# Hybrid decoder block: a new written order for all engines up to the first attention step, with one pair's weight sums on VectorE

## Chip, cores, metric

One core of one Trainium2 chip. The metric is the device time of one execution in microseconds (us). The engines are named as in the profile: PE (TensorE), DVE (VectorE), ACT (ScalarE), POOL (GpSimd), SP (SyncE, which issues the DMAs).

## The reference

One decoder layer on a 1024 x 1024 float32 input, one batch:

```python
h = rmsnorm(x, mix_norm_g[l])
proj = h @ w_in[l]
qa, ka, va, q_lat, kv_lat, k_r, g_a, g_b = jnp.split(proj, IN_OFFSETS, axis=-1)
qa = apply_rope(qa.reshape(B, S, SWA_HEADS, HEAD_DIM), cos_a, sin_a)
ka = apply_rope(ka.reshape(B, S, SWA_KV_HEADS, HEAD_DIM), cos_a, sin_a)
o_a = swa_sink_attention(qa, ka, va, swa_sinks[l])        # 8 heads of 64, window 128
cq = rmsnorm(q_lat, q_norm_g[l])                          # 384 wide
ckv = rmsnorm(kv_lat, kv_norm_g[l])                       # 256 wide
...
y = jax.nn.sigmoid(g_a) * (o_a @ w_o_swa[l]) + jax.nn.sigmoid(g_b) * (o_b @ w_o_mla[l])
x = x + y @ w_out[l]
h = rmsnorm(x, ffn_norm_g[l])
x = x + (jax.nn.silu(h @ w_gate[l]) * (h @ w_up[l])) @ w_down[l]
return rmsnorm(x, final_norm_g)
```

`o_b` is latent attention over `cq` and `ckv` with a separate rotary key.

## The kernel before

**Arithmetic.** Every float32 factor is split into a high part and a low part. ScalarE writes the high part (a copy or cast), VectorE the low part (the value minus the high part). `mm3` (L164 to L170) then runs three matmuls for each block of 128 rows: high by high (L168), high by low (L169 or L170, by operand) and low by high. In the large products, a 2 x 2 arrangement of half matrices is computed with seven products instead of eight, in the order 1, 6, 2, 7, 5, 4, 3. That needs sums and differences of weight tiles (`lat_mix`, `lat_mix2`, and in class `Seven` `mix` and a part of `prep`), which GpSimd makes, and of activation tiles ("sets": `set_sub` on VectorE, `set_four` on GpSimd). A product is 12 matmuls of 512 columns.

**Stages.** First comes the projection to the local attention's queries, keys and values (`nat`, L505 to L516: 8 row blocks, two column groups, two parts of 12 matmuls of 336 columns each). For each block, `square` takes the sum of squares on ScalarE and a 128 x 128 diagonal `dg` of the norm factors on GpSimd (L438), `spread` multiplies it with ones on TensorE (`rb`, L442), and `normalize` multiplies the transposed block on VectorE (L445). Behind the projection `row_act` and `row_dve` (L472, L479) apply the rotation; the five VectorE instructions of the latter are the lines L489 to L498 and two of L173 and L176. Then come the latent projections: three pairs j = 0, 1, 2 of seven products each (tiles `fa`, `fb`, weights `wr`, sums `sm`, split weights `wl`; casts at L871, low parts at L873). Then the gates (class `Seven`, object `gates`) are woven into 16 steps of local attention (`for it in range(N_SW)`): query transposes `qT`, scores `sc`, softmax, transposes of the probabilities `pT`, values. Behind these lie latent attention, the output product and the feed-forward part.

**What sets the order.** The string `ROWS` is an order written out by hand for all five engines. It is executed while the kernel is built, one step after the other, and each engine runs its instructions in just this order. A step is two letters and indices; `STEPS` (L1031) maps the letters to functions: `nt` nat, `xs`/`xt` loads, `sq` square, `sp` spread, `nm` normalize, `qh`/`ql` high and low part of a normalized block, `ho` its store, `ra`/`rd` rotation on ScalarE and VectorE, `qo` store of the queries, `sl` load of a set, `ss` its three subtractions, `sf` set_four, `sh`/`so` high and low part of a set's tile, `la`/`sc` load and scale of latent weights, `mx`/`my` the two parts of their sums, `lh`/`ll` high and low part of latent weights, `mm` a latent product, `ev` its copy out of the accumulator, `es` its square sum, `rh`/`rl`/`ro` split and store of a result, `kr` the rotary key, `kl` load of the keys, `gl`/`gs`/`gm`/`gp` load, scale, sums and preparation of the gates' weights, `wq`/`wt`/`ws` load, transposes and scores of an attention step. An engine that reaches an instruction whose operand is late waits there, and all that stands behind it on that engine waits too. Behind `ROWS` the attention loop and what follows run in the order of the code; `lat_tail` puts the latent results' norms between the loop's steps by their number, the first of it, `lat_stats`, with 32 matmuls of one column (`st`, L1053).

Of the kernel before, what the change touches and what calls it, by code (L numbers as in the profile page):

```python
# [8 lines left out]
F32 = mybir.dt.float32  # L9
# [8 lines left out]
P = 128  # L18
# [69 lines left out]
def hybrid_block_kernel(  # L88
# [475 lines left out]
    def set_four(c):  # L564
        if c // 2 not in t4_raw:
            t4_raw[c // 2] = U("h4", F32, (P, 2, 4, P))
        r, t = h_set[c]
        for k in range(0, 4, 2):
            k = slice(k, k + 2)
            sub(t4_raw[c // 2][:, c % 2, k], r[:, 1, k], t[:, 1, k], nc.gpsimd)  # L570
# [6 lines left out]
        sq0 qh2 xs2 sq1 ql2 nt110 xt7 ra0 xs4 qh3 sp0 rd0 nt111 xt4 sp1 ra1 ql3 xt5 nt200 sq2 qo0 nm0 nt201 xs3 rd1  # L577
        qh0 xs6 nt210 sq4 xs7 ql0 sp2 nt211 xt6 nm2 xs5 nm1 sp4 ra2 nt300 ho2 sq3 nm4 nt301 sq6 qo1 rd2 ho4 qh4 nt310
        ho0 qh2 ql4 la10 qh1 sp6 nt311 ql2 sq5 qo2 ho1 ql1 nt400 ra3 sq7 rd3 sp5 nt401 nm5 qo3 sp7 nt410 tb nm7 qh5
        ho5 sc10 nt411 nm6 ho7 ql5 qh6 ho6 sp3 nm3 qh7 nt500 la01 ra4 ql7 qh3 ho3 nt501 lh11 ql6 sl1 nt510 ll11 rd4  # L580
        sl2 nt511 ql3 nt600 ra5 sc01 qo4 rd5 la00 nt601 sl0 ns ss1 nt610 la11 nt611 sh12 sf1 ss2 qo5 sl3 nt700 ra6
        so12 sh22 sf2 sc00 rd6 nt701 mx0 nt710 ss0 qo6 sc11 nt711 so22 sh02 so02 ra7 lh01 rd7 sf0 ll01 mx1 ph qo7 sh23
        ss3 sh14 mm01 sh13 sh03 sh21 so23 sh31 sh32 so13 mm11 kt1 ev01 so03 lh06 so32 sh33 sf3 ll06 sh01 sh04 so31
        mm06 lh02 so01 lh07 ll02 ev11 so04 sh34 my0 sh11 so34 mm02 lh05 ev06 sh24 ll07 so33 so11 la20 mm07 ev02 so21
        es02 ll05 lh16 so14 ll16 la21 mm05 lh03 ev07 ll03 so24 kt0 mm16 lh04 ev05 ll04 kr05 sc20 mm03 lh12 ev16 rh05
        sc21 ll12 mm04 rl05 my1 ev03 ro05 lh21 es03 ll21 mx2 mm12 lh17 ev04 ll17 kr04 gl00 mm21 lh22 ll22 rh04 ev12
        rl04 es12 my2 mm17 ev21 ro04 lh26 rh12 ll26 rl12 mm22 lh15 ev17 ro12 gs00 ll15 wq0 kl gp1 mm26 ev22 lh27 es22
        ll27 rh22 rl22 mm15 lh13 ev26 ll13 gl01 mm27 lh25 ev15 ro22 ll25 es15 rh15 mm13 wq1 ev27 rl15 lh14 ro15 ll14
        wt0 lh23 ev13 gl10 mm25 ll23 rh13 es13 rl13 gs01 mm14 ev25 ro13 lh24 gm0 es25 ll24 mm23 ev14 es14 rh14 rl14
        ws0 ev23 ro14 es23 mm24 gp2 gp3 rh23 rr rl23 ev24 ro23 es24  # L590
    """

    class Seven:


        def __init__(self, pairs, ms, load, done, ahead, load_at, mix_at, head=(), at=None, scale=None, scale_at=(), piece=4, vec=()):


            self.pairs, self.ms, self.load, self.done = pairs, ms, load, done
            self.n_ahead = ahead  # L600
            j0 = 1 + max((j for j, _ in head), default=-1)
            order = list(head) + [(j, q) for j in range(j0, pairs) for q in ORDER]
# [9 lines left out]
            self.scaled = set()  # L612
            self.scale = scale
# [32 lines left out]

        def prep(self, j, q, m):
# [5 lines left out]
            if q == 7:  # L653
                a12, s1 = self.part(j, m, 1, 0), self.sums[(j, m)][:, 1]
                for k in range(0, 4, self.piece):
                    k = slice(k, k + self.piece)
                    sub(a12[:, k], a12[:, k], s1[:, k], nc.gpsimd)
# [14 lines left out]
        def run(self):  # L672
            j, q, m = self.seq[self.n_run]
# [8 lines left out]
            if q == 6:  # L682
# [4 lines left out]
                go_on=q in (2, 7, 4, 3))  # L687
            if q == 1:
                self.tmp[(j, m)] = U("pu", F32, (P, 2, 512))
# [12 lines left out]
            return j, q, m  # L702
# [41 lines left out]
    def sw_qT(it):  # L744
# [5 lines left out]
        ptq = ptq.bitcast(F32)  # L750
        qs = U("qs", F32R, (P, 2, 2, P))
        e, o = qs[:, :, 0], qs[:, :, 1]
        nc.scalar.copy(e[0:64], ptq[0:64])
        nc.scalar.copy(o[64:128], ptq[64:128])
        nc.vector.tensor_tensor(e[64:128], ptq[0:64], e[0:64].bitcast(F32), op=ALU.subtract)
        nc.vector.tensor_tensor(o[0:64], ptq[64:128], o[64:128].bitcast(F32), op=ALU.subtract)
        d["qs"] = qs

    def sw_scores(it):
        g, b = divmod(it, NB)  # L760
        d = sw[it]
        qs = d.pop("qs")
        c0 = P if b == 0 else 0
        kc = slice((b - 1) * P + c0, (b + 1) * P)
        mx = tiny("mx", 4)
        scs = []
        for hp in range(2):
            sc = PX("sc", (P, 2, 2 * P))
            scs.append(sc)
            for j in range(2):  # L770
                nc.tensor.matmul(sc[:, j, c0:], qs[:, hp, j], khd[g][0][:, kc], start=True, stop=False)
                nc.tensor.matmul(sc[:, j, c0:], qs[:, hp, j], khd[g][1][:, kc], start=False, stop=True)
            for j in range(2):
                h = 2 * hp + j
                nc.vector.tensor_tensor_reduce(sc[:, j, c0:], sc[:, j, c0:], band[:, c0:], 1.0, NEG, op0=ALU.add,
                                               op1=ALU.max, accum_out=mx[:, h:h + 1])
# [4 lines left out]
        nc.vector.tensor_tensor(es, nm, ns, op=ALU.subtract)  # L781
        den = tiny("den", 4)
# [16 lines left out]
        d["kbs"] = [1] if b == 0 else [0, 1]  # L799

# [47 lines left out]
    def lat_mix(j):  # L848
        a11, a21, a22 = lraw[(j, 0)][:, :, 0], lraw[(j, 0)][:, :, 1], lraw[(j, 1)][:, :, 1]
        t = lsum[j] = U("sm", F32, (P, 2, 4, P))  # L850
        for k in range(0, 4, 2):
            k = slice(k, k + 2)
            add(t[:, 0, k], a21[:, k], a22[:, k], nc.gpsimd)
            sub(t[:, 1, k], t[:, 0, k], a11[:, k], nc.gpsimd)
            sub(a21[:, k], a11[:, k], a21[:, k], nc.gpsimd)

    def lat_mix2(j):
        a12 = lraw[(j, 1)][:, :, 0]
        for k in range(0, 4, 2):
            k = slice(k, k + 2)  # L860
            sub(a12[:, k], a12[:, k], lsum[j][:, 1, k], nc.gpsimd)
# [165 lines left out]
    def small_tables():  # L1027
# [10 lines left out]
             "ws": sw_scores}  # L1038
# [45 lines left out]
    lat_tail = {0: lat_stats, 1: lat_diag, 2: lambda: lat_norm(0), 3: lambda: kv_split(0), 4: lambda: (kv_store(0), lat_norm(1)),  # L1084
                5: lambda: kv_split(1), 6: lambda: kv_store(1)}
    pool_order = tc.manual_schedule(engines={engines.Pool})
    pool_order.__enter__()
    for it in range(N_SW):
        if it + 2 < N_SW:
            sw_q(it + 2)  # L1090
        if it == 0:
            sw_qT(1)
        gate_step()
        if it >= 1:
            sw_pT(it - 1)
            if it + 1 < N_SW:
                sw_qT(it + 1)
# [3 lines left out]
        if it >= 1:  # L1101
            sw_pv(it - 1)
# [1016 lines left out]
```

## Time and profile before

| | us |
|---|---|
| runs | 1333.82, 1336.08, 1337.1 (median 1336.08) |
| profiled execution | 1336.97 |
| its span | 1335.1 |
| granted TensorE clock, mean of the span | 0.994 |

The times of rows are those of the profiled execution, in microseconds from the start of its span; 1.87 us of its time lie around the span. A row of a timeline gives start, duration, engine, line, operation, written tile <- read tiles, shape, the number of equal instructions joined in the row, and in brackets the idle time of the engine ahead of it with what ended it. In a row of waits stand the engine, what waited, who was waited for, the total, how often, and the longest. A window's row gives the busy time of each engine in a stretch, the granted clock (1.00 is full speed) and the share of the DMA engines in use. Matmuls overlap, so that their pitch, from start to start, is shorter than one matmul's duration.

### The profile page before, as it was taken

How to read it: one execution, taken by the hardware profiler on the slowest of the kernel's cores; microseconds unless marked ns; L12 is line 12 of the kernel's file. 1: busy time of each engine (PE TensorE's matmuls, PEld its weight loads, DVE VectorE, ACT ScalarE, POOL GpSimd, SP SyncE). 2: the span in 40 equal slices, each digit the busy share in tenths (PEclk: the TensorE clock that was granted, in tenths of full speed). 3: DMA queues.
4: the chain of work that ended last, by engine and by line, in shares of the span. 5: the costliest groups of instructions: out<-in, count | busy, mean ns of one | idle time of the engine just before them, and what ended most of it. 6: DMA issues, size and time to landing. Idle time of an engine off the chain costs nothing.

```text
span 1335.1 us, 18710 instructions
## 1 busy us (share of the span) xinstructions
PE 1310.3 (98%) x6368; PEld 1094.8 (82%) x6368; DVE 927.5 (69%) x1450; ACT 643.2 (48%) x1281; POOL 592.4 (44%) x629
## 2 busy tenths in 40 slices
PE   9989999999999999999999999999999999999997
PEld 7967787788888888888888888888888888888886
DVE  7997587787658767876879756566755564664863
ACT  6555466675347667764356323322233233644452
POOL 3364855464135455503142555777666541022521
PEclk9989999999999999999999999999999999999999
DMA  9927336444777557798522234556543425996503
GB/s 358 344 86 212 104 130 220 167 146 178 248 253 221 127 176 173 205 385 204 176 102 95 86 144 170 193 206 239 185 160 141 169 97 194 376 386 228 174 18 141
DMA packets 93456, 254.22 MB, mean 190 GB/s; under 512 B 10416, under 2 KB 16176, under 8 KB 91312
## 3 DMA queue, kind: packets, MB, share of 16 engines
q1 hardware_dynamic: 88496, 242.35, 51.8%
q0 software_dynamic: 3424, 8.39, 3.6%
q10 hardware_dynamic: 1440, 2.27, 0.5%
q8 instruction: 51, 0.84, 0.3%
q14 instruction: 45, 0.37, 0.1%
HBM read 166.60 MB, written 82.18 MB: 186 GB/s over the span
## 4 chain that ended last, share of the span: by engine, by line
PE 65%; DVE 1%; issue 1%; ACT 0%; POOLq 0%; POOL 0%; DVEq 0%; ACTq 0%
PE fa L170 6%; PE fa L168 6%; PE fa L169 6%; PE fd L169 5%; PE fd L168 5%; PE fd L170 5%; PE fb L169 4%; PE fb L170 4%; PE fb L168 4%; PE xo L170 2%; PE xo L169 2%; PE xo L168 2%; PE pTb L1282 2%; PE oB L170 1%; PE oB L169 1%; PE oB L168 1%
## 5 line engine op out<-in xcount | busy, mean ns | idle before, releaser
L162 DVE TENSOR_TENSOR wl<-wr,wl 128x512 fp32r<-128x512 f32 x150 | 144.9, 989 | 72.0 <-ACT wl L159 71.5
L162 DVE TENSOR_TENSOR lrv<-lr,lrv 128x1024 fp32r<-128x1024 f32 x77 | 105.5, 1402 | 48.4 <-ACT lrv L159 46.0
L159 ACT CAST lrv<-lr 128x1024 fp32r<-128x1024 f32 x77 | 80.2, 1052 | 90.2 <-PE fd L170 57.3
L173 POOL TENSOR_TENSOR wr<-wr,sm 128x256 f32<-128x256 f32 (+1 forms) x44 | 55.0, 1261 | 148.9 <-DVE wl L162 120.0
L168 PE MATMUL fd<-lrv 128*128 128x512 f32 x308 | 119.8, 389 | 0.0
L169 PE MATMUL fd<-lrv 128*128 128x512 f32 x308 | 119.8, 389 | 0.0
L170 PE MATMUL fd<-lrv 128*128 128x512 f32 x308 | 119.8, 389 | 0.0
L159 ACT CAST wl<-wr 128x512 fp32r<-128x512 f32 x150 | 86.7, 620 | 3.1 <-DVE t3l L173 2.8
L1267 POOL TENSOR_TENSOR denb<-denb,neg_one 128x1 f32<-128x1 f32 x64 | 41.4, 647 | 87.5 <-ACT p L1266 66.1
L162 DVE TENSOR_TENSOR wl<-sm,wl 128x512 fp32r<-128x512 f32 x60 | 49.3, 844 | 43.5 <-ACT wl L159 41.6
L168 PEld LDWEIGHTS fd<-lrv 128*128 128x128 f32 x308 | 57.8, 188 | 12.1
L170 PEld LDWEIGHTS fd<-lrv 128*128 128x128 f32 x308 | 57.8, 188 | 12.0
L169 PEld LDWEIGHTS fd<-lrv 128*128 128x128 f32 x308 | 57.8, 188 | 11.8
L1266 ACT ACTIVATE p<-scb,nmb 128x384 f32<-128x384 f32 (+3 forms) x64 | 47.7, 746 | 32.9 <-DVE nmb L1265 21.7
L1265 DVE CUSTOM_DVE_ANT_0 scb<-scb,mask,rlat 128x384 f32<-128x384 f32 (+3 forms) x64 | 52.1, 819 | 13.5 <-PE scb L1257 12.5
L168 PE MATMUL fa<-hh,wl 128*128 128x512 f32 x132 | 53.9, 408 | 3.5 <-ACT wl L871 3.5
L170 PE MATMUL fa<-hh,wl 128*128 128x512 f32 x132 | 53.3, 404 | 3.8 <-DVE wl L173 3.8
L1640 ACT ACTIVATE act<-sm 128x512 f32<-128x512 f32 x11 | 7.0, 633 | 101.7 <-DVE sm L176 101.7
L162 DVE TENSOR_TENSOR ptl<-pTb,pth 128x512 fp32r<-128x512 f32 (+2 forms) x96 | 49.9, 550 | 7.4 <-ACT pth L159 7.1
L169 PE MATMUL fa<-hl,wl 128*128 128x512 f32 x132 | 52.9, 401 | 0.0
L173 POOL TENSOR_TENSOR wr<-wr 128x256 f32<-128x256 f32 (+1 forms) x42 | 52.6, 1253 | 0.0
L168 PE MATMUL fb<-t2h,wl 128*128 128x512 f32 x132 | 51.8, 392 | 0.7 <-ACT wl L159 0.7
(352 smaller groups left out, 4147.3 us busy)
## 6 DMA issues: line engine op xcount, KB each, us to landing
lr<-la_d SPq DMA_DIRECT2D x77, 256.0 KB, 5.6
wr<-in_w_gate_dram SPq DMA_DIRECT2D x22, 512.0 KB, 3.9
wr<-in_w_up_dram SPq DMA_DIRECT2D x22, 512.0 KB, 4.9
la_d<-sd SPq DMA_DIRECT2D x22, 512.0 KB, 5.5
wd<-in_w_down_dram SPq DMA_DIRECT2D x22, 512.0 KB, 6.9
rb_d<-wd SPq DMA_DIRECT2D x22, 512.0 KB, 2.6
lr<-rb_d SPq DMA_DIRECT2D x44, 256.0 KB, 5.8
lr<-in_w_down_dram SPq DMA_DIRECT2D x33, 256.0 KB, 5.2
```

The costliest lines, as they stand in the source:

```text
L159: i = nc.scalar.copy(hi, src)
L162: (eng or nc.vector).tensor_tensor(lo, src, hi.bitcast(F32), op=ALU.subtract)
L168: nc.tensor.matmul(ps, ah, bh, start=first and i == 0, stop=False, skip_group_check=go_on)
L169: nc.tensor.matmul(ps, ah, bl, start=False, stop=False, skip_group_check=go_on)
L170: nc.tensor.matmul(ps, al, bh, start=False, stop=last and i == n - 1, skip_group_check=go_on)
L173: eng.tensor_tensor(out, a, b, op=ALU.subtract)
L1265: nc.vector.tensor_tensor_reduce(s_, s_, m_, rlat[:, n:n + 1], -NEG, op0=ALU.add, op1=ALU.min, accum_out=nm)
L1266: nc.scalar.activation(p_, s_, AF.Exp, scale=-1.0, bias=nm, accum_out=den)
L1267: nc.gpsimd.tensor_tensor(den, den, neg_one[:, 0:1], op=ALU.pow)
L1282: nc.tensor.transpose(pp[:, i], p[:, blk(k0 + i)], ident)
L1640: nc.scalar.activation(dst, src, AF.Silu)
```

## The change

The string `ROWS` is a new one, and reaches further: the first local attention step (`it = 0`), which the loop ran before, is now written into it, and the loop begins at 1. For this some functions are cut in pieces that can be placed one by one: the attention step's query transposes, its high and low part, the products, maxima, shift and exponentials; in `Seven` the product and its copy out, and the second weight sum (`lower`). `lat_tail` begins one step later. `lat_mix`, `lat_mix2` and `set_four` take an engine and a piece size; the steps `mX1` and `mY2` put the sums of pair 1 and the second sum of pair 2 on VectorE, in one piece each (three and one instruction of 128 x 512 where GpSimd had six and two of 128 x 256). GpSimd has 547 rows of instructions instead of 555, VectorE 1430 instead of 1426; TensorE has the same instructions in another order. From TensorE's row 793 on, inside the first attention steps, the order is that of before, on every engine alike.

```diff
-        sq0 qh2 xs2 sq1 ql2 nt110 xt7 ra0 xs4 qh3 sp0 rd0 nt111 xt4 sp1 ra1 ql3 xt5 nt200 sq2 qo0 nm0 nt201 xs3 rd1
...
-        so12 sh22 sf2 sc00 rd6 nt701 mx0 nt710 ss0 qo6 sc11 nt711 so22 sh02 so02 ra7 lh01 rd7 sf0 ll01 mx1 ph qo7 sh23
...
+        qh2 sq0 ql2 sq1 xs4 nt110 qh3 xt6 ql3 nt111 ra0 xs2 rd0 xt4 sp1 ra1 sp0 sq4 xs6 nm0 nt200 nm1 qo0 qh0 ho0
...
+        ra6 sc00 so22 sf3 rd6 nt701 qo5 sh32 qo1 so32 mx0 qo6 nt710 so12 nt711 lh01 ll01 ra7 mm01 rd7 tb qo2 my0 lh06
...
+        def lower(self, j, m):
+            if (j, m) in self.lowered:
+                return
+            self.lowered.add((j, m))
+            a12, s1 = self.part(j, m, 1, 0), self.sums[(j, m)][:, 1]
+            for k in range(0, 4, self.piece):
+                k = slice(k, k + self.piece)
+                sub(a12[:, k], a12[:, k], s1[:, k], nc.gpsimd)
...
+            step = self.product()
+            self.copy_out(*step)
+            return step
...
-    def lat_mix(j):
+    def lat_mix(j, eng=nc.gpsimd, n=2):
         a11, a21, a22 = lraw[(j, 0)][:, :, 0], lraw[(j, 0)][:, :, 1], lraw[(j, 1)][:, :, 1]
         t = lsum[j] = U("sm", F32, (P, 2, 4, P))
-        for k in range(0, 4, 2):
-            k = slice(k, k + 2)
-            add(t[:, 0, k], a21[:, k], a22[:, k], nc.gpsimd)
...
+        for k in range(0, 4, n):
+            k = slice(k, k + n)
+            add(t[:, 0, k], a21[:, k], a22[:, k], eng)
+            sub(t[:, 1, k], t[:, 0, k], a11[:, k], eng)
+            sub(a21[:, k], a11[:, k], a21[:, k], eng)
...
+             "gy": lambda j: gates.lower(j, "g"), "gx": lambda n: gates.product(),
+             "ge": lambda n: gates.copy_out(*gates.seq[n - 1]), "wu": sw_q_hi, "wv": sw_q_lo,
+             "wr": lambda it: sw_products(it, range(2)), "wm": lambda it: (sw_max(it, range(2)), sw_shift(it)),
+             "we": sw_exp, "no": lambda it: sw[it].pop("norm")(), "mv": lambda it: nc.sync.dma_start(*sw[it].pop("move")),
+             "mX": lambda j: lat_mix(j, nc.vector, 4), "mY": lambda j: lat_mix2(j, nc.vector, 4),
...
-    lat_tail = {0: lat_stats, 1: lat_diag, 2: lambda: lat_norm(0), 3: lambda: kv_split(0), 4: lambda: (kv_store(0), lat_norm(1)),
+    lat_tail = {1: lat_stats, 2: lat_diag, 3: lambda: lat_norm(0), 4: lambda: kv_split(0),
...
-    for it in range(N_SW):
+    for it in range(1, N_SW):
```

VectorE at the projection's end, before: the last set subtractions (`hr`, `ht`), two low parts (`t2l`), the rotation of block 7 (`rp`, `vv`, `qn`), and in the last row the low part of the first latent product's weights (`wl`).

```order
L173 TENSOR_TENSOR ht_772<-ht_772 128x512
L173 TENSOR_TENSOR ht_772<-ht_772,hr_771 128x512
L173 TENSOR_TENSOR t2l_806<-ht_712,t2h_805 128x4x128
L173 TENSOR_TENSOR t2l_806<-ht_772,t2h_805 128x4x128
L489 TENSOR_TENSOR rp_910<-n_820,ra_154 128x512 x2
L494 TENSOR_TENSOR vv_174<-n_820,vv_174 128x2x64
L173 TENSOR_TENSOR qn_911<-rp_910 128x8x32
L176 TENSOR_TENSOR qn_911<-rp_910 128x8x32
L173 TENSOR_TENSOR wl_908<-wr_757,wl_908 128x512
```

VectorE at the same place in the changed kernel: the rotation ahead of the first latent low part is that of block 6, and that of block 7 (`rp_919`) follows behind it.

```order
L489 TENSOR_TENSOR rp_842<-n_744,ra_154 128x512 x2
L494 TENSOR_TENSOR vv_174<-n_744,vv_174 128x2x64
L173 TENSOR_TENSOR qn_843<-rp_842 128x8x32
L176 TENSOR_TENSOR qn_843<-rp_842 128x8x32
L173 TENSOR_TENSOR t2l_739<-ht_732,t2h_738 128x4x128
L173 TENSOR_TENSOR t2l_739<-ht_651,t2h_738 128x4x128
L173 TENSOR_TENSOR wl_901<-wr_759,wl_901 128x512
L489 TENSOR_TENSOR rp_919<-n_820,ra_154 128x512 x2
```

The rotation of block 7 has moved behind `wl`; the fourth set's subtractions, which came behind `wl` before, now stand ahead of these rows.

ScalarE at the latent products' end, before: the scale of gate weights (`gT`) stands ahead of the last cast (`wl_1400`) for a latent product.

```order
L871 CAST wl_1356<-wr_1062 128x512
L940 ACTIVATE cs_1375<-pu_1011,latg 128x512
L931 ACTIVATE sqt_1377<-pu_1011 128x512
L717 ACTIVATE wr_1306<-wr_1306,gT 128x256 x4
L871 CAST wl_1400<-wr_1062 128x512
```

ScalarE in the changed kernel: the last three casts for latent products (L925), results and square sums, and then the gates' scales (L733) with a cast of gate weights (L159).

```order
L925 CAST wl_1309<-wr_1166 128x512
L925 CAST wl_1314<-sm_1234 128x512
L925 CAST wl_1317<-sm_1234 128x512
L994 ACTIVATE cs_1320<-pu_1126,latg 128x512
L985 ACTIVATE sqt_1336<-pu_1126 128x512
L985 ACTIVATE sqt_1340<-fa_1145 128x512
L994 ACTIVATE cs_1344<-fa_1145,latg 128x512
L994 ACTIVATE cs_1361<-pu_1126,latg 128x512
L985 ACTIVATE sqt_1363<-pu_1126 128x512
L733 ACTIVATE wr_1312<-wr_1312,gT 128x256 x4
L159 CAST wl_1383<-wr_1312 128x512
L733 ACTIVATE wr_991<-wr_991,gT 128x256 x4
```

The scale has moved behind all casts for the latent products.

More of the change, by code (lines that the diff above doesn't have):

```diff
@@ L612, in __init__ @@
             self.scaled = set()
+            self.lowered = set()
             self.scale = scale
@@ L653, in prep @@
             if q == 7:
[L654 to L657, printed above, removed]
+                self.lower(j, m)
             t = U("wl", F32R, (P, 2, 4, P))
@@ L672, in run, with product @@
         def run(self):
+            step = self.product()
+            self.copy_out(*step)
+            return step
+        def product(self):
             j, q, m = self.seq[self.n_run]
@@ L687, in run, with copy_out @@
                 go_on=q in (2, 7, 4, 3))
+            return j, q, m
+        def copy_out(self, j, q, m):
+            ps = self.acc[("A" if q in (1, 2, 5, 3) else "B", j, m)]
             if q == 1:
@@ L799, in sw_scores, with sw_qT_all @@
         d["kbs"] = [1] if b == 0 else [0, 1]
+    def sw_scores(it):
+        for hp in range(2):
+            sw_products(it, [hp])
+            sw_max(it, [hp])
+        sw_shift(it)
+        sw_exp(it)
+    def sw_qT_all(it):
+        sw_qT(it)
+        sw_q_hi(it)
+        sw_q_lo(it)
     def sw_pT(it):
```

101 lines of the change are left out of this document (58 added, 43 removed).

## The prediction

> **What bounds the kernel now.** I read the page's busy shares first, then the windows by stage, then TensorE's waits, and last the timeline of each engine around them. The page's first part:
>
> ```profile
> PE 1310.3 (98%) x6368; PEld 1094.8 (82%) x6368; DVE 927.5 (69%) x1450; ACT 643.2 (48%) x1281; POOL 592.4 (44%) x629
> ```
>
> TensorE (PE) works for 1310.3 of the span's 1335.1 us, so all that an order can win is 24.8 us of idle time and the matmuls that run at a lower granted clock. The windows say where both lie (the columns are start:end, length, busy time and count of PE, PE loads, VectorE, ScalarE and GpSimd, then granted clock, DMA share and GB/s):
>
> ```profile
> 69.40:75.60 6.20, 0.77 (x3) 0.30 (x2) 6.20 (x10) 3.98 (x9) 5.38 (x6) 0.84 0.05 18
> 75.60:91.50 15.90, 15.76 (x58) 12.52 (x59) 15.83 (x21) 9.26 (x18) 12.13 (x8) 0.85 0.35 111
> ...
> 129.70:150.90 21.20, 17.37 (x80) 13.19 (x79) 13.36 (x32) 11.92 (x30) 16.58 (x23) 1.00 0.33 122
> 150.90:159.30 8.40, 8.40 (x51) 7.31 (x50) 1.76 (x5) 3.23 (x12) 4.65 (x4) 0.80 0.50 142
> ...
> 241.40:1335.10 1093.70, 1082.23 (x5221) 905.88 (x5220) 739.48 (x1086) 496.89 (x926) 470.91 (x465) 1.00 0.55 186
> ```
>
> Behind 241.40 TensorE is busy for 1082.23 of 1093.70 us, in an order that the change leaves as it is (from the first attention steps on, the same rows on every engine). What the change can touch are two places: the end of the first projection (69.40 to 75.60: TensorE busy for 0.77 us, VectorE for all 6.20), and the end of the latent products (129.70 to 150.90: 21.20 − 17.37 = 3.8 us idle). TensorE's waits up to 250 us name them (total, times, longest):
>
> ```profile
> PE fa L170 <- DVE wl L173: 3.8, 1, 3.8
> PE fa L168 <- ACT wl L871: 3.5, 2, 1.9
> ...
> PE sc L771 <- DVE qs L755: 1.1, 1, 1.1
> PE fb L168 <- ACT wl L159: 0.7, 1, 0.7
> ...
> PE rb L442 <- POOL dg L438: 0.2, 1, 0.2
> ```
>
> And TensorE's timeline shows them in place (start, duration, what; the wait before it in brackets):
>
> ```profile
> 69.12 0.32 PE L516 MATMUL n<-wv,hl 128*128 128x336 f32 x1
> 71.06 0.50 PE L168 MATMUL fa<-hh,wl 128*128 128x512 f32 x1 [1.63 <-ACT wl L871]
> ...
> 75.63 0.80 PE L170 MATMUL fa<-hh,wl 128*128 128x512 f32 x1 [3.84 <-DVE wl L173]
> ...
> 80.07 0.55 PE L168 MATMUL fa<-hh,wl 128*128 128x512 f32 x1
> ...
> 91.56 0.39 PE L168 MATMUL fa<-t1h,wl 128*128 128x512 f32 x1
> ...
> 94.28 0.39 PE L168 MATMUL fb<-t2h,wl 128*128 128x512 f32 x1
> ...
> 134.81 0.22 PE L771 MATMUL sc<-khd,qs 128*128 128x128 f32 x1
> ...
> 135.65 0.45 PE L168 MATMUL fb<-t4h,wl 128*128 128x512 f32 x1
> ...
> 146.83 0.39 PE L771 MATMUL sc<-khd,qs 128*128 128x256 f32 x1 [1.14 <-DVE qs L755]
> ...
> 148.17 0.40 PE L168 MATMUL fa<-hh,wl 128*128 128x512 f32 x1
> ...
> 150.92 3.63 PE L1053 MATMUL st<-neg_one,sq 128*128 128x1 f32 x32
> 154.41 0.49 PE L168 MATMUL fb<-t3h,wl 128*128 128x512 f32 x1
> ...
> 158.79 0.50 PE L809 MATMUL pT<-ident_r,per 128*128 128x128 f32 x4
> ```
>
> A product is 12 matmuls of 512 columns; at full clock it takes 94.28 − 91.56 = 2.72 us, 0.227 each. The first latent product begins at 71.06 with the high part of its weights, stops for the low part until 75.63, and then needs 80.07 − 75.63 = 4.44 us for ten matmuls, 2.17 more than ten times 0.227; the granted clock of these windows is 0.84 and 0.85. So this place costs 1.63 + 3.84 + 2.17 = 7.6 us. [...]
>
> **Part by part: the projection's end.** The question is when VectorE finishes the low part of the first latent product's weights, called T here; it is 74.37 + 1.21 = 75.6 now. VectorE's rows (ropes L489, normalization L445, the set subtractions and the low parts L173):
>
> ```profile
> 40.31 1.29 DVE L489 TENSOR_TENSOR rp<-n,ra 128x512 f32<-128x512 f32 x2 [1.56 <-ACT ra L477]
> ...
> 51.61 1.28 DVE L489 TENSOR_TENSOR rp<-n,ra 128x512 f32<-128x512 f32 x2
> ...
> 53.67 1.29 DVE L173 TENSOR_TENSOR hl<-xt,hh 128x512 fp32r<-128x512 f32 x2
> ...
> 57.33 0.69 DVE L173 TENSOR_TENSOR hr<-ht,hr 128x512 f32<-128x512 f32 x1
> ...
> 59.40 0.68 DVE L173 TENSOR_TENSOR hr<-ht,hr 128x512 f32<-128x512 f32 x1
> 60.11 1.12 DVE L173 TENSOR_TENSOR ht<-ht 128x512 f32<-128x512 f32 x1
> ...
> 74.37 1.21 DVE L173 TENSOR_TENSOR wl<-wr,wl 128x512 fp32r<-128x512 f32 x1
> ...
> 82.36 0.68 DVE L173 TENSOR_TENSOR t2l<-ht,t2h 128x512 fp32r<-128x512 f32 x1
> ```
>
> Undisturbed, a rope step takes 53.67 − 51.61 = 2.06 us, a set's three subtractions 59.40 − 57.33 = 2.07 (0.69 each), a low part 1.29 / 2 = 0.645. From 60.11 on the same instruction takes 1.12 to 1.21, because GpSimd works beside it:
>
> ```profile
> 59.62 2.21 POOL L173 TENSOR_TENSOR h<-hr,ht 128x256 f32<-128x256 f32 x2 [16.85 <-DVE ht L173]
> ...
> 64.24 0.73 POOL L176 TENSOR_TENSOR sm<-wr,wr 128x256 f32<-128x256 f32 x1
> ...
> 79.55 2.33 POOL L173 TENSOR_TENSOR h<-hr,ht 128x256 f32<-128x256 f32 x2
> ```
>
> From the first to the last of these GpSimd ran 20 instructions (eight for the four sets, twelve for two mixes). Between 60.11 and 82.36 VectorE issued eight set subtractions, seven low parts and two ropes, undisturbed 5.52 + 4.5 + 4.12 = 14.1 us; they took 22.25. So a GpSimd instruction charges VectorE 8.1 / 20 = 0.41 us.
>
> From the rope of block 4 on, the new order has up to T: three ropes (4, 5, 6; the rope of block 7 now comes behind T), four sets instead of three, and eight low parts instead of six. That is 6.2 + 8.3 + 5.2 = 19.6 us, against 8.2 + 6.2 + 3.9 = 18.3 before, and 14 GpSimd instructions (four sets, one mix) stand ahead, 5.7 us at 0.41. The start of that rope was 51.61. Three normalizations now stand ahead of the rope that waits 1.56 us at 40.31, so I take 1.2 us off, 50.4; the bounds are 50.0 and 51.6. T = 50.4 + 19.6 + 5.7 = 75.7, the 75.6 of before. What rope 7 leaves, the added set and low parts fill. Bounds: 70.0 with no charge at all, 80.5 where each GpSimd instruction charges its whole 0.73. I take the middle value, since it is this same pair of engines at this same place: **0.0 us**, wait and half clock stay.
>
> [...] The trace shows the slowing (0.69 to 1.12 and more), but a charge of 0.41, not 0.73; as a rival it is priced below.
>
> After T both orders run five products up to 91.56; only which ones differs, and the low parts that they need are made earlier now: 0.
>
> **The latent products' end.** From 91.56 to 150.92 are 59.36 us. In them lie 19 products (16 latent, 3 of the gates), 51.7 us at 2.72, and the scores of two attention steps, 135.65 − 134.81 = 0.84 and 148.17 − 146.83 = 1.34. The rest is 5.5 us of loss, of which 3.7 us are the three waits in the list (1.9, 1.1, 0.7; the other 1.6 of the 3.5 is the 71.06 row). The longest comes from ScalarE:
>
> ```profile
> 129.71 1.71 ACT L717 ACTIVATE wr<-wr,gT 128x256 f32<-128x256 f32 x4 [1.42 <-DMA ct_d<-cs]
> 131.32 0.60 ACT L871 CAST wl<-wr 128x512 fp32r<-128x512 f32 x1
> ```
>
> The scale of gate weights (L717) stands ahead of the cast for the last latent products and itself waits for its load; TensorE starts at 131.97, behind both. In the new order the last latent casts stand ahead of that scale, so this wait goes, with nothing late behind it but the gates' products, which now come later. The 0.7 (gate weights' high part) and the 1.1 (scores behind the query's high and low part) go since a gate product now stands between the query's transposes and its scores: 2.72 us of cover for 1.1; without it the 1.1 is back. I leave 0.5 us for the transposes and for new short waits (a query split behind a GpSimd sum). **Gain 5.0**; bounds 2.5 (only the waits, with a new one of the size of the 1.1 row) and 5.5.
>
> **The rest.** Pair 1's mix on VectorE is three 128x512 instructions, 2.1 us at 0.69, and pair 2's second mix one, 0.7; they fall where VectorE has idle time (busy 13.36 of 21.20 in the fourth window), so 0, and 2.8 if that cover were gone. GpSimd's six and two instructions go: 0. The split of the attention step into pieces issues the same instructions: 0. The 32 narrow matmuls at 150.92 are followed by a product that takes 158.79 − 154.41 = 4.38 us, 1.66 too many, at clock 0.80; they come one attention step later now, and what follows them will be slow as here: 0, bounds ±1.7, since the dip may fall on fewer or more matmuls.
>
> Sum: −5.0 us. The profiled execution took 1336.97 us (1.87 around its span), so 1332.0 in its frame; the median of the three runs shown is 0.9 lower: **1331.1**. A measurement here tells about 0.3% from no change, 4.0 us: faster is below 1332.1, slower above 1340.1.
>
> **Rivals.**
> B, the gap at the projection's end shrinks too. If VectorE gets to T by 72.5, the wait is 3.1 us shorter and too short for the half clock: 3.1 + 2.2 = 5.3 more, 1325.8. For it: VectorE, busy for all of the window, decides there, and rope 7 moved out. Against: 1.3 us of uncontended work were added. Chance 0.18.
>
> C, the hand order's waits are replaced. A fixed order stops an engine at every late operand; with two new waits of the 1.1 to 1.9 kind the gain is 5.0 − 3.0 = 2.0: 1334.1. For it: ScalarE, VectorE and GpSimd all get a new order in this stretch. Against: I find no instruction standing ahead of its operand there. Chance 0.20.
>
> E, each GpSimd instruction blocks VectorE for its whole 0.73: 14 times 0.32 more, T at 80.2, 4.5 us of wait added: 1335.6. Against: the 0.41. Chance 0.07.
>
> D, slower: the projection starves. It needs one diagonal from GpSimd for each block's spread, and those rows differ sixfold:
>
> ```profile
> 26.24 2.20 POOL L438 TENSOR_SCALAR dg<-ident_r,rn 128x128 f32<-128x128 f32 x1
> ...
> 29.44 0.37 POOL L438 TENSOR_SCALAR dg<-ident_r,rn 128x128 f32<-128x128 f32 x1
> ```
>
> The new order moves the spreads. Where four diagonals fall beside VectorE's runs of subtractions and each is 1.83 late, TensorE loses 7.3 us and, at one of them, the 2.2 of the half clock: 9.5 − 5.0 = 4.5 slower, 1340.6. It decides from three late ones on (5.5 against 5.0). Against: TensorE now waits for a diagonal once, 0.2 us (the last row of its waits). Chance 0.09.
>
> A, my forecast, has the other 0.46.
>
> **The numbers.** Range: down to B less the 1.7 of the dip, 1324.5 (rounded up); upward to E with part of the same dip, 1337.0; what is left out is D and the edges of B and E, 0.2 together. Faster by over 0.3%: A lies only 1 us beyond the bound, three quarters of it (0.345), B (0.18), a bit of C: 0.54. Slower: most of D, 0.07. Within: 0.39.
>
> **What would show it.** Right: TensorE stops again at the first latent product, until 75 to 77, with matmuls at twice their pitch behind it; no wait of over 0.5 us between then and the narrow matmuls; ScalarE's gate scale behind the last latent cast. Wrong: a first low part that ends before 73 (B), a new wait row of over 1 us in the latent products (C), one past 79 (E), or `rb` waits before 69 (D).

## The result, and the profile after

The changed kernel takes 1325.91 us (median; 1322.89 to 1328.84), the kernel before 1336.08 (1333.82 to 1340.26): a ratio of 0.992, with a 95% interval of 0.9895 to 0.9944. The profiled executions stand at 1336.97 and 1325.91, spans 1335.1 and 1323.7: 11.4 us less in the span.

The page's first part, and the windows of the changed kernel (columns as above):

```profile
PE 1304.4 (99%) x6368; PEld 1094.1 (83%) x6368; DVE 928.3 (70%) x1454; ACT 644.1 (49%) x1281; POOL 578.4 (44%) x621
```

```profile
69.40:75.60 6.20, 3.69 (x20) 3.03 (x19) 6.20 (x9) 0.51 (x3) 6.04 (x8) 0.96 0.33 108
75.60:91.50 15.90, 15.90 (x65) 12.99 (x65) 14.87 (x25) 14.87 (x31) 0.54 (x1) 0.91 0.74 256
...
129.70:150.90 21.20, 20.58 (x96) 16.46 (x97) 12.58 (x26) 13.03 (x35) 16.08 (x24) 1.00 0.28 98
150.90:159.30 8.40, 8.40 (x57) 7.64 (x56) 4.93 (x16) 3.84 (x13) 3.51 (x5) 1.00 0.32 103
```

TensorE's idle time falls by 5.5 us (24.8 to 19.3), and its busy time by 5.9 us with the same 6368 matmuls, at a mean granted clock of 0.996 instead of 0.994. The two together are the 11.4 us. Its waits up to 250 us:

```profile
PE fa L170 <- DVE wl L173: 2.5, 1, 2.5
PE rb L442 <- POOL dg L438: 1.4, 1, 1.4
...
PE fb L168 <- DVE sm L176: 1.2, 1, 1.2
PE sc L793 <- DVE qs L780: 0.4, 1, 0.4
```

The first latent product still stops for its low part, but for 2.5 us instead of 3.8; a spread waits 1.4; the three waits at the latent products' end have gone but for 0.4, and one of 1.2 is new. Windows at equal clock times compare different work, though. To see where the time went, I took the starts of instructions that close the same work in both kernels: the sixth product; the probabilities' transposes of the loop step `it = 2`, behind the 32 narrow matmuls in both; and the transposes six steps on. TensorE's timeline of the changed kernel:

```profile
74.21 0.50 PE L170 MATMUL fa<-hh,wl 128*128 128x512 f32 x1 [2.51 <-DVE wl L173]
...
75.30 0.63 PE L168 MATMUL fa<-hh,wl 128*128 128x512 f32 x1
...
77.86 0.63 PE L168 MATMUL fb<-t2h,wl 128*128 128x512 f32 x1
...
89.10 0.39 PE L168 MATMUL fb<-t4h,wl 128*128 128x512 f32 x1
...
121.97 0.22 PE L793 MATMUL sc<-khd,qs 128*128 128x128 f32 x1
...
129.85 0.50 PE L168 MATMUL fb<-t4h,wl 128*128 128x512 f32 x1 [1.20 <-DVE sm L176]
...
148.74 0.29 PE L863 MATMUL pT<-ident_r,per 128*128 128x128 f32 x2
...
164.09 0.29 PE L863 MATMUL pT<-ident_r,per 128*128 128x128 f32 x2
...
232.43 0.37 PE L863 MATMUL pT<-ident_r,per 128*128 128x128 f32 x3
```

And of the kernel before, the two marks that were not shown, and the wait that lies between them:

```profile
169.71 0.37 PE L809 MATMUL pT<-ident_r,per 128*128 128x128 f32 x3
...
234.77 0.50 PE L821 MATMUL o<-ptl,vv 128*128 128x512 f32 x1 [1.21 <-DVE ptl L162]
...
244.21 0.37 PE L809 MATMUL pT<-ident_r,per 128*128 128x128 f32 x3
```

| stretch of equal work | before | changed | gain | foreseen |
|---|---|---|---|---|
| to the end of five latent products | 91.56 | 89.10 | 2.46 | 0 |
| to the transposes behind the narrow matmuls | 78.15 | 74.99 | 3.16 | 5.0 |
| six attention steps | 74.50 | 68.34 | 6.16 | 0 |
| the rest of the span | 1090.9 | 1091.3 | −0.4 | 0 |

More than half of the gain in these two executions lies in the six attention steps, which the prediction took for unchanged. But the change also moves the latent norms (`lat_tail`) by a step, and these lie in just these steps.

Each column is one execution, and one execution can stray. The run e9 below has the order of the kernel before up to 217 us, and yet it needs 80.03 us for the second stretch (from 92.32 to 172.35) where the kernel before needed 78.15. A gain of 3.16 us in that stretch can therefore not be told from one of 5.

### The profile page after: what moved, and what is told of

It reads as the page before. It is cut to its first block, busy times and chain, and to the rows that moved or that the text cites. A ratio compares the mean times of both kernels' runs of the same rounds, so it can differ in the third digit from the quotient of the medians.

```text
span 1323.7 us, 18707 instructions
## 1 busy us (share of the span) xinstructions
PE 1304.4 (99%) x6368; PEld 1094.1 (83%) x6368; DVE 928.3 (70%) x1454; ACT 644.1 (49%) x1281; POOL 578.4 (44%) x621
## 4 chain that ended last, share of the span: by engine, by line
PE 66%; DVE 1%; issue 1%; ACT 0%; POOLq 0%; POOL 0%; DVEq 0%; ACTq 0%
PE fa L170 6%; PE fa L169 6%; PE fa L168 6%; PE fd L168 5%; PE fd L169 5%; PE fd L170 5%; PE fb L170 5%; PE fb L169 5%; PE fb L168 5%; PE xo L169 2%; PE xo L170 2%; PE xo L168 2%; PE pTb L1337 2%; PE oB L170 1%; PE oB L169 1%; PE oB L168 1%
## 5 line engine op out<-in xcount | busy, mean ns | idle before, releaser
L159 ACT CAST lrv<-lr 128x1024 fp32r<-128x1024 f32 x77 | 80.2, 1052 | 90.0 <-PE fd L170 58.6
L173 POOL TENSOR_TENSOR wr<-wr,sm 128x512 f32<-128x512 f32 (+1 forms) x42 | 49.1, 1179 | 160.8 <-DVE wl L162 121.2
L159 ACT CAST wl<-wr 128x512 fp32r<-128x512 f32 x150 | 86.5, 620 | 3.3 <-DVE t3l L173 2.8
L168 PE MATMUL fb<-t4h,wl 128*128 128x512 f32 x132 | 51.7, 392 | 1.2 <-DVE sm L176 1.2
L159 ACT CAST pth<-pTb 128x512 fp32r<-128x512 f32 (+2 forms) x96 | 43.3, 480 | 18.8 <-PE pTb L1337 18.3
```

The source lines that it names most:

```text
L159: i = nc.scalar.copy(hi, src)
L168: nc.tensor.matmul(ps, ah, bh, start=first and i == 0, stop=False, skip_group_check=go_on)
L173: eng.tensor_tensor(out, a, b, op=ALU.subtract)
```

## The experiments

Each run has its own measurements of the kernel before; the ratio is to those, with its 95% interval. "Steps" is the length of the six attention steps in its profile, by the marks of the table: 74.50 before, 68.34 changed.

| run | median us | ratio | steps |
|---|---|---|---|
| e1 norms late, old order | 1337.25 | 1.0006 (0.9995 to 1.0018) | 68.35 |
| e2 norms early, new order | 1328.72 | 0.9933 (0.9918 to 0.9948) | 71.99 |
| e3 sums on GpSimd | 1326.19 | 0.992 (0.9905 to 0.9935) | 68.30 |
| e4 rotation 7 late, old order | 1338.95 | 1.0016 (1.0007 to 1.0024) | 72.42 |
| e5 second norm early | 1325.25 | 0.9927 (0.9907 to 0.9947) | 68.27 |
| e6 sets late | 1325.10 | 0.992 (0.9902 to 0.9939) | 68.27 |
| e7 gate preparation late | 1327.03 | 0.9929 (0.9915 to 0.9942) | 68.33 |
| e8 gate scale late, old order | 1334.36 | 0.9986 (0.9974 to 0.9998) | 71.89 |
| e9 kv_split late, old order | 1333.04 | 0.9965 (0.9954 to 0.9976) | 69.28 |
| e10 low parts late | 1325.62 | 0.9915 (0.99 to 0.993) | 68.56 |
| e11 query early | 1323.97 | 0.9905 (0.9889 to 0.9922) | 68.64 |
| e12 query and maxima early | 1323.11 | 0.9909 (0.9895 to 0.9923) | 68.25 |

**The attention steps: the norms late in the old order (e1), early in the new one (e2).**

```diff
-    lat_tail = {0: lat_stats, 1: lat_diag, 2: lambda: lat_norm(0), 3: lambda: kv_split(0), 4: lambda: (kv_store(0), lat_norm(1)),
-                5: lambda: kv_split(1), 6: lambda: kv_store(1)}
+    lat_tail = {1: lat_stats, 2: lat_diag, 3: lambda: lat_norm(0), 4: lambda: kv_split(0),
+                5: lambda: (kv_store(0), lat_norm(1)), 6: lambda: kv_split(1), 7: lambda: kv_store(1)}
```

> The kernel before, with only the latent norms (lat_tail) one attention step later. Theory S (the steps from 165 to 245 us got 6.2 us shorter in the changed kernel because kv_split and its neighbours moved by a step): the waits of TensorE for ptl (0.37 at 221, 1.21 at 235) and the half clock behind the second go, 5 to 6 us faster, about 1330.5. Rival R (they went because the new order leaves ScalarE, VectorE and the loads further ahead when the loop begins, and the place of the norms is nothing): the waits stay, within 1 us of 1336.

e2 is the reverse edit on the changed kernel, with `lat_stats` called just ahead of the loop.

> The changed kernel, with only the latent norms back at the steps they had before (the statistics ahead of the loop). Theory S: the ptl waits come back, 5 to 6 us slower than the changed kernel, about 1331.5. Rival R: no ptl wait, within 1 us of 1326. A mixed answer (a short wait without the half clock) would say that both are needed.

In e1 the steps fall from 74.50 to 68.35 us, and in e2 they rise from 68.34 to 71.99, with one of the two waits back (e2's waits of TensorE):

```profile
PE o L875 <- DVE ptl L162: 1.2, 1, 1.2
```

So the place of the norms decides on that wait in both orders. In the new order it does not bring back the half clock (0.51 from 237.35 to 240.70 in the kernel before): the product behind the wait takes 2.8 us in e2, at full pitch. That is the mixed answer which e2's expectation names, 3.65 us in the steps instead of 6. And e1 as a whole gains nothing. TensorE's timeline of e1, ahead of the steps:

```profile
156.86 0.73 PE L809 MATMUL pT<-ident_r,per 128*128 128x128 f32 x4 [2.78 <-DMA per<-pe]
```

The 32 narrow matmuls (3.63 us), which stood here before, had covered the round trip of the first step's probabilities through memory. With them moved on, TensorE waits 2.8 us for that load, and further waits follow (1.2 for a cast of gate weights). The steps begin at 177.76 instead of 169.71, and these 8.05 us take back what the steps win. In the changed kernel the first step's scores come at 122 instead of 135 us, its probabilities are there in time, and the transposes at 148.74 do not wait. So the move of all the norms needs the first attention step early: alone it is worth nothing. The reverse is not so. Without the move of the norms the new order is still faster than the kernel before, with a ratio of 0.9933 (8.2 us by the medians), and taking the norms back costs 1.7 us by the ratios (0.9933 and 0.992), which is not clear of noise since the intervals overlap, and 3.65 us in the profiled steps.

**Which of the norms it is (e5, e9).**

```diff
-    lat_tail = {1: lat_stats, 2: lat_diag, 3: lambda: lat_norm(0), 4: lambda: kv_split(0),
-                5: lambda: (kv_store(0), lat_norm(1)), 6: lambda: kv_split(1), 7: lambda: kv_store(1)}
+    lat_tail = {1: lat_stats, 2: lat_diag, 3: lambda: lat_norm(0), 4: lambda: (kv_split(0), lat_norm(1)),
+                5: lambda: kv_store(0), 6: lambda: kv_split(1), 7: lambda: kv_store(1)}
```

> The changed kernel, with only the second half's lat_norm one attention step earlier, kv_split where the change put it. It splits what the run with all norms early showed (3.6 us of waits and slow matmuls back in the steps of 163 to 235 us). Theory N (it is lat_norm(1): its two VectorE instructions of 0.7 us then stand in a step in which VectorE also serves a gate sum): those steps take 70 to 72 us, not 68.3. Theory K (it is kv_split(1): two casts and two subtractions ahead of the probabilities' split on ScalarE and VectorE): 68.3 us, as in the changed kernel.

The steps take 68.27 us, as in the changed kernel: it is not `lat_norm(1)`. e9 moves only `kv_split(1)` and its store, in the kernel before:

```diff
-                5: lambda: kv_split(1), 6: lambda: kv_store(1)}
+                6: lambda: kv_split(1), 7: lambda: kv_store(1)}
```

> The kernel before, with only the second half's kv_split (and its store) one attention step later; statistics and both lat_norms stay. Theory K: this alone takes the ptl waits and the slow matmuls out of the steps from 170 to 244 us, 74.5 us before, 68.3 to 69 with it: 5 to 6 us faster, about 1331, with no wait for the probabilities' load, since the 32 narrow matmuls stay where they cover it. Rival: it takes all the norms together, the steps stay at 72 us or more, under 3 us faster.

The steps take 69.28 us, and the medians fall by 4.7 us (1337.7 to 1333.04): in the old order this one-line edit is worth nearly half of what the whole change brings. TensorE's timeline of e9 at the sixth product and at the two marks of the steps (between these it waits for no `ptl`):

```profile
92.32 0.39 PE L168 MATMUL fa<-t1h,wl 128*128 128x512 f32 x1
...
172.35 0.38 PE L809 MATMUL pT<-ident_r,per 128*128 128x128 f32 x3
...
241.63 0.37 PE L809 MATMUL pT<-ident_r,per 128*128 128x128 f32 x3
```

How two casts and two subtractions do this can be read in the kernel before. VectorE, in the two steps concerned:

```profile
217.91 1.29 DVE L162 TENSOR_TENSOR cs<-klr,cs 128x512 fp32r<-128x512 f32 x2
219.11 0.88 DVE L162 TENSOR_TENSOR wl<-wr,wl 128x512 fp32r<-128x512 f32 x1
219.92 0.68 DVE L176 TENSOR_TENSOR go<-fa,sm 128x512 f32<-128x512 f32 x1
220.52 1.27 DVE L162 TENSOR_TENSOR ptl<-pT,pth 128x512 fp32r<-128x512 f32 x2
...
233.43 0.69 DVE L176 TENSOR_TENSOR pu<-fb,pu 128x512 f32<-128x512 f32 x1 [2.13 <-ACT wl L159]
234.03 1.28 DVE L162 TENSOR_TENSOR ptl<-pT,pth 128x512 fp32r<-128x512 f32 x2
```

`kv_split` (`cs`, 1.29) stands ahead of the probabilities' low part (`ptl`) in a step in which VectorE also copies out a gate product (`go`). TensorE waits 0.37 us at 221.25, its scores come later, so do the maxima, the exponentials and the casts behind them on ScalarE; in the next step a copy-out (`pu`) and `ptl` start only at 233.43, TensorE waits 1.21 at 234.77, and the clock behind it falls, to 0.78 over this window of the kernel before:

```profile
233.50:241.40 7.90, 6.58 (x24) 4.93 (x24) 5.73 (x18) 5.03 (x17) 1.18 (x4) 0.78 0.62 241
```

That chain is read from the rows; what the runs show is that moving `kv_split(1)` ends it.

**The sums of two pairs on VectorE (e3).**

```diff
-... sc20 mX1 wq0 ...   ... ev15 mY2 lh27 ...
+... sc20 mx1 wq0 ...   ... ev15 my2 lh27 ...
```

> The changed kernel, with the sums of pair 1 and the second sum of pair 2 back on GpSimd, at the same places of the order. Theory of the prediction (they lie beside TensorE's work on either engine): within 1 us of 1326. Rival: VectorE's 2.8 us for them are cheaper than GpSimd's eight instructions that hold up VectorE and the casts behind them: a new wait of TensorE between 92 and 150 us of 1 to 3 us, 1327 to 1329.

1326.19 us, ratio 0.992 as for the changed kernel: the engine makes no difference that these runs can tell. The sums did not fall into the window that the prediction named, though: in the changed kernel they ran at 93 us, where VectorE is busy for 16.04 of the 18.50 us from 91.5 to 110, and at 112 us.

**The projection's end (e4, e6, e10).** e4, in the kernel before:

```diff
-... lh01 rd7 sf0 ll01 mx1 ...
+... lh01 sf0 ll01 rd7 mx1 ...
```

> The kernel before, with only the rotation of block 7 moved behind the first latent low part on VectorE. Theory of the prediction (VectorE alone sets that point, and its work is what counts): the low part is done 2.6 to 3.1 us earlier, at 72.5 to 73.0 instead of 75.6, the wait before it 0.7 to 1.2 us instead of 3.84, and with a short wait no or half of the slow matmuls behind it: 3 to 5 us faster, 1331 to 1333. Rival (another late operand, such as the cast of these weights or a set, stands right behind): under 1 us faster.

It is slower, by 0.16%. The wait for the first low part fell to 1.2 us as the theory has it, but the second product then waited for a tile of the sets, and more behind it (e4's waits):

```profile
PE fb L169 <- DVE t2l L173: 2.2, 1, 2.2
```

e6, in the changed kernel:

```diff
-... ss3 sh22 sf2 nt700 ra6 sc00 so22 sf3 rd6 ...   ... qo2 my0 lh06 ...
+... ss3 sh22 nt700 ra6 sc00 so22 rd6 ...   ... qo2 my0 sf2 sf3 lh06 ...
```

> The changed kernel, with GpSimd's part of the third and fourth set (four instructions) moved behind the first two weight sums, so that they run after the first latent low part instead of ahead of it. Theory of the prediction (a charge of about 0.4 us on VectorE for each): the low part is done 1.7 us earlier, at 72.4, TensorE's wait there 0.8 us instead of 2.5, and with so short a wait none of the slow matmuls: 3 us faster, 1323. Rival E (each blocks VectorE for its whole 0.73): 2.9 us earlier, 4 us faster, 1322. Rival: the tiles of t4 are late then, a wait of 1 us or more before the sixth product: no gain.

The wait fell only from 2.5 to 2.2 us, and the median stayed where it was, by neither of the rivals: GpSimd's sums, which stood behind the four moved instructions, started at 66.31 instead of 68.86 and held VectorE in their place: the low part at 66.49 took 1.23, the one at 66.92 in the changed kernel 0.68. VectorE's rows of the changed kernel show what the unit of the charge is:

```profile
56.24 0.68 DVE L173 TENSOR_TENSOR hr<-ht,hr 128x512 f32<-128x512 f32 x1
56.96 1.11 DVE L173 TENSOR_TENSOR ht<-ht 128x512 f32<-128x512 f32 x1
...
67.52 1.28 DVE L489 TENSOR_TENSOR rp<-n,ra 128x512 f32<-128x512 f32 x2
68.72 0.28 DVE L494 TENSOR_TENSOR vv<-n,vv 128x128 fp32r<-128x128 f32 x1
68.91 0.96 DVE L173 TENSOR_TENSOR qn<-rp 128x256 f32<-128x256 f32 x1
```

And e6's rows, first VectorE's and then GpSimd's, show it without the four instructions: GpSimd stands idle for 5.14 us up to 66.31, and the fourth set's subtraction takes 0.69 (1.12 in the changed kernel, at 64.72).

```profile
65.16 0.69 DVE L173 TENSOR_TENSOR ht<-ht 128x512 f32<-128x512 f32 x1
...
67.64 1.28 DVE L489 TENSOR_TENSOR rp<-n,ra 128x512 f32<-128x512 f32 x2
```

```profile
66.31 0.86 POOL L176 TENSOR_TENSOR sm<-wr,wr 128x256 f32<-128x256 f32 x1 [5.14 <-ACT wr L900]
```

A subtraction `ht` of two SBUF tiles takes 1.11 instead of 0.69 while GpSimd works, a low part such as `wl` 1.21 instead of 0.69, and `qn` 0.96 instead of 0.42; the rotation's products from PSUM (`rp` from `n`) stay at 0.64 each. So the price goes by VectorE's instructions that start while GpSimd works, 0.42 to 0.54 us each, and the two rotations whose products ran beside GpSimd (at 59.14 and 67.52) paid nothing for them: 1.27 and 1.28 for the pair, and 1.28 at 50.31, where GpSimd stood idle. The whole-instruction charge of rival E, 0.73 each, is in none of these rows.

e10, in the changed kernel:

```diff
-... qo1 so32 mx0 qo6 nt710 so12 nt711 lh01 ll01 ra7 mm01 rd7 tb qo2 my0 lh06 ph lh07 ll06 sh03 ...
+... qo1 mx0 qo6 nt710 nt711 lh01 ll01 so32 so12 ra7 mm01 tb qo2 my0 lh06 ph lh07 ll06 rd7 sh03 ...
```

> The changed kernel, with two low parts of set tiles (blocks 1 and 3 of t2) moved from ahead of the first latent low part to just behind it, and the rotation of block 7 behind the second product's low part. Theory (VectorE's work ahead of that point sets TensorE's wait, and what stands behind it has time): the low part is done 2.3 us earlier, the wait 0.2 instead of 2.5 us, no slow matmuls behind it: 3 to 4 us faster, 1322.5. Rival (VectorE is full in the whole stretch, so that the wait only moves to the second product, as when the rotation alone was moved): under 1 us.

The first wait went (0.3), and a wait of the same size came for the second product (e10's waits):

```profile
PE fb L168 <- DVE vv L494: 2.3, 1, 2.3
...
PE fa L170 <- DVE wl L173: 0.3, 1, 0.3
```

Its accumulator (`fb`) is the buffer of block 7's projection, which the rotation of block 7 had not yet read (`vv` is its last read). Of the three moves none won: VectorE is busy for 27.52 of the 28 us from 50 to 78, and TensorE's stop changed its place (e4, e10) or stayed (e6). By these rows, what can shorten the stop is less VectorE work in the stretch, an earlier start, or less contention; the change had the last two (the sum stands in the next section).

**The latent products' end (e8, e7, e11, e12).** e8, in the kernel before:

```diff
-... rl13 gs01 mm14 ev25 ro13 lh24 gm0 ...
+... rl13 mm14 ev25 ro13 lh24 gs01 gm0 ...
```

> The kernel before, with only the scale of the second half of the gates' weights on ScalarE moved behind the last latent cast. Theory of the prediction: the wait of 1.85 us at 132 goes, and with the restart 2 us are won, 1334 to 1334.5. Rival: it comes back in the waits that stand behind it (0.74 for the gates' high part, 1.14 for the scores), under 1 us.

It is faster by 1.9 us by the ratio (0.9986, interval 0.9974 to 0.9998), but not where either theory had it. The cast came earlier, and TensorE waited at the same place for something else, which in the kernel before had ended at the same moment (VectorE, e8's first row and before's second; each is the copy-out that frees the accumulator):

```profile
131.90 0.69 DVE L176 TENSOR_TENSOR klr<-fa,sm 128x512 f32<-128x512 f32 x1 [3.00 <-DMA ct_d<-cs]
```

```profile
131.13 0.69 DVE L176 TENSOR_TENSOR klr<-fa,sm 128x512 f32<-128x512 f32 x1 [2.57 <-DMA ct_d<-cs]
```

The same wait for `klr` stands in e9 (2.2 us), which leaves the scale in its place: the cast and the copy-out end within 0.1 us of each other, and which of them is last differs between executions. The waits named in this stretch sum to 3.07 us instead of 3.73. Yet e8 reaches the steps at 171.10, 1.39 us later than the kernel before, and wins 2.61 us in the steps (71.89), which it did not touch. So where its 1.9 us come from, these profiles do not show.

e7 takes up the new wait of 1.2 us of the changed kernel. Its cause stands in ScalarE's and VectorE's rows there:

```profile
123.93 1.71 ACT L733 ACTIVATE wr<-wr,gT 128x256 f32<-128x256 f32 x4 [2.45 <-DMA wr<-in_w_gt_dram]
125.67 0.62 ACT L159 CAST wl<-wr 128x512 fp32r<-128x512 f32 x1
```

```profile
126.32 0.76 DVE L162 TENSOR_TENSOR wl<-wr,wl 128x512 fp32r<-128x512 f32 x1 [3.46 <-ACT wl L159]
...
129.12 0.68 DVE L176 TENSOR_TENSOR sm<-fb,pu 128x512 f32<-128x512 f32 x1
```

It is the pattern of before, one engine on: a gate scale waits for its load, VectorE's low part waits for its cast, and the copy-out (`sm`) that TensorE needs stands behind it.

```diff
-... wr0 ev26 gp1 mm27 gl11 gm0 wm0 gs10 wq1 we0 mm25 ev27 mm24 ...
+... wr0 ev26 mm27 gl11 gm0 wm0 gs10 wq1 we0 mm25 ev27 gp1 mm24 ...
```

> The changed kernel, with the preparation of the first gate weights (a cast on ScalarE and a low part on VectorE that waits 3.5 us for it, since its scale waits for a load) moved behind the maxima and the copy-out of latent product 27. Theory: that low part stands in VectorE's queue ahead of the copy-out for which TensorE waits 1.2 us at 129.85; the wait and the slow restart go, 1.3 to 1.5 us faster, 1324.5. Rival: the gate product behind it then starts late instead, within 0.5 us of 1326.

The 1.2 went, but the run is no faster than the changed kernel: the wait for the second query's split grew from 0.4 to 2.0 (e7's waits):

```profile
PE sc L793 <- DVE qs L780: 2.0, 1, 2.0
```

e11 moves that query ahead as well:

```diff
-... ev27 mm24 wq2 ev25 no0 gp2 es25 mm23 gp3 ev24 es24 gy0 mv0 wt1 ev23 gx1 wu1 wv1 es23 ...
+... ev27 gp1 mm24 wt1 wq2 ev25 wu1 no0 wv1 gp2 es25 mm23 gp3 ev24 es24 gy0 mv0 ev23 gx1 es23 ...
```

> The changed kernel, with the first gate weights' preparation behind the copy-out of product 27, as in the earlier run, and the second query's transposes with their split moved ahead by one product, ahead of the second gate weights' cast. Theory (each of these waits is a matter of what stands ahead in ScalarE's and VectorE's queues): both the wait of 1.2 us at 129.85 and the wait for the query's split (0.4, or 2.0 in the earlier run) go, 2 to 2.5 us faster than the changed kernel, 1323.5 to 1324. Rival: a gate product comes late in their place, within 0.5 us.

Both waits went, and one of 2.7 us came at 144.67, for the copy-out of a gate product behind the maxima. e12 moves the maxima too (`wm1` from behind `gx2` to behind `wr1`):

> The run before (query early) with one more step moved: the maxima of the second step's scores ahead of a result's split and of the third gate product's preparation. There TensorE waited 2.7 us at 145 for the copy-out of the second gate product, which stood on VectorE behind the maxima, and these behind a low part that waited 1.8 us for its cast. Theory: the wait goes, with nothing in its place, 2.7 us faster than that run and 4 faster than the changed kernel, 1321.5. Rival (VectorE and ScalarE are so full here that each change of the order moves the wait on): another wait of 1 us or more between 130 and 165 us, 1323.5 to 1326.

The wait fell to 1.6 (e12's waits):

```profile
PE fb L168 <- DVE pu L176: 1.6, 1, 1.6
```

e11 and e12 have the lowest medians of all, 1323.97 and 1323.11, but their intervals overlap with that of the changed kernel (0.9895 to 0.9944): that they are faster than it is not shown.

## Why the prediction was right, and where it was wrong

The sign was right and the time lies in the range, 5.2 us below the forecast and close to rival B's 1325.8. But it came there by another way than B's, and in good part by luck: of the three stretches that gained, the forecast had counted on one. By its own signs it was not borne out either, since TensorE resumed at 74.21 (75 to 77 was named) and a wait of 1.20 us came before the narrow matmuls (none over 0.5 was named).

- **The steps: the term that failed.** That TensorE keeps its order behind 241.40 is true, but "from the first attention steps on, the same rows on every engine" is not, neither there nor where the change is described: the norms stand a step later, on TensorE up to the second norm's matmuls (201.53 us before, 206.95 changed), and on VectorE up to `kv_split(1)` (217.91 before, 221.79 changed), the very instructions that counted. The only part of them that I priced was the narrow matmuls (0 ± 1.7), and that came out: the product behind them takes 4.44 us, 4.38 before. The two `ptl` waits at 221 and 235 us, and the half clock behind the second, were in the trace, and I took them to stay. Foreseen 0, measured 6.16 in the profiled executions; e9 gives 5.2 to the place of `kv_split(1)` in the old order, and e2 gives 3.65 to that of all the norms in the new one.
- **The projection's end.** That VectorE's work sets T was right; the unit of GpSimd's charge was not. T was foreseen at 75.7; it is 74.2 (the low part starts at 72.95):

```profile
50.31 1.28 DVE L489 TENSOR_TENSOR rp<-n,ra 128x512 f32<-128x512 f32 x2
...
72.95 1.21 DVE L173 TENSOR_TENSOR wl<-wr,wl 128x512 fp32r<-128x512 f32 x1
74.08 1.28 DVE L489 TENSOR_TENSOR rp<-n,ra 128x512 f32<-128x512 f32 x2
```

The start, 50.31, was foreseen at 50.4. Of the 23.85 us up to 74.16 the uncontended work is the 19.6 of the prediction, so the charge is 4.25 us instead of 5.7. I had spread it over GpSimd's instructions; it goes by VectorE's that start beside them (four subtractions, two `qn` and three low parts, raised by 4.3 us together), and two of the three ropes read PSUM beside GpSimd. T came 1.4 us earlier: 1.3 by the earlier start and 1.4 by the smaller charge, less 1.3 of added work. The wait is 1.3 us shorter (3.84 to 2.51) and the slow matmuls behind it fewer (granted clock 0.50 from 75.63 to 80.07 before, 0.63 from 74.21 to 77.86 changed): 2.46 us in all. That a wait of 0.7 us is too short for the half clock (rival B) no run shows at this place: in e4 the pitch is 0.43 us behind a wait of 1.25 (one of 2.01 lies two matmuls ahead of it), in e10 it is 0.23 behind one of 0.26. At the latent products' end of the kernel before, the clock is 1.00 in the window with the waits of 1.85, 0.74 and 1.14. (The upper bound of the prediction, 80.5, is 80.2 by its own terms.)
- **The latent products' end.** The gain was 3.16 instead of 5.0, a difference that single executions cannot settle, as said. The waits of 1.85 and 0.74 us went, the 1.14 fell to 0.42, and a new one of 1.20 came, which is rival C's mechanism at half its price. "So this wait goes, with nothing late behind it but the gates' products" was wrong in two ways. In the old order a second operand was as late as the cast, a copy-out that waited for a store (e8); the changed kernel escapes both. And the gate's scale that waits for its load still stands ahead of something that TensorE needs, by way of VectorE (e7). For the kernel before, the prediction said that the scale waits for its load; the row names the store `ct_d<-cs` instead, and no run tells which of the two it was.
- **The sums on VectorE** at 0 and the engine's indifference: right (e3).
- **Rival D** showed in part: a spread waits 1.4 us for its diagonal at 39 us. By these rows it cost nothing: the first latent product began at 71.08, as before (71.06), since the 1.63 us wait for the cast, which lay there before, was gone, and T came later still. It would begin to cost if T came earlier.

What stays open: e2, e4 and e8, with the norms in their old place, have 72 us in the steps and not 74.5. In their timelines the same `ptl` wait of 1.21 us is there, but the product behind it takes 2.8 us, where the kernel before needs 4.40: 1.6 us of the difference is whether the clock falls behind that wait. Why it falls in one and not in the others, no run shows. So of the 6.16 us some 1.6 may be chance of the profiled execution; 4.7 by the medians of e9 is the surer figure for that move, and it holds for the old order. How the gain of the new order without the norms (e2) divides between the projection's end and the latent products' end is read from rows; no run undid the one without the other.

## What to carry to other kernels

Compare the order over the whole stretch before a term is set to zero: here the largest one came from a table of two lines behind the long one, and in the old order a single moved entry was worth nearly half of the whole gain. Where an engine is full over a stretch, as VectorE was here for 27.52 of 28 us, moving an instruction of it, or of GpSimd beside it, need not shorten TensorE's stop: in three runs the stop changed its place (2.2 us in e4, 2.3 in e10) or stayed (2.2 in e6). And where a wait names one releaser, look for a second operand that ends just before it. One edit can need another: what a moved filler had covered, here a load that TensorE then waited 2.78 us for, must be early first (e1). Before a gain is given to a stretch, look how much the same stretch differs between two executions of one order.

## What the runs showed of the hardware

- A VectorE subtraction of two SBUF tiles (128 x 512) takes 0.69 us alone and 1.11 to 1.23 us where it starts while GpSimd works, beside GpSimd's instructions of 0.79 to 1.19 us; the rotation's products of the same size, with one operand in PSUM, took 0.64 each with GpSimd at work and without.
- The slow matmuls behind a stop vary, here and behind the `ptl` wait above. Behind the narrow matmuls the next product took 4.44 us in the changed kernel (at a granted clock of 0.62), 2.87 in e5, and 5.27 in e10, all in the same place of the order: up to 2.4 us of difference, though neither edit touches the order there.
